# A two-block network on one Trainium2 core: other filler beside the RWKV recurrence, and linear attention's rows kept on chip

## The chip, the cores and the metric
The kernel runs on one core of a Trainium2 chip. The core has five engines, each with its own queue of instructions that it works off in order: TensorE (PE; its weight loads are shown apart as PEld), VectorE (DVE), ScalarE (ACT), GpSimd (POOL) and SyncE (SP), which issues most of the transfers. Engines wait for each other through semaphores. The metric is device time of one execution in microseconds (us); the profile of one execution gives its span from the first to the last instruction.

## The reference
Two blocks over 512 tokens of width 1024, in float32:

```python
# first block
p = rmsnorm(x, norm1_g) @ w_in
p_rwkv, q, k, v, gate_logits = jnp.split(p, IN_SPLITS, axis=-1)
y_a = rwkv7_bidirectional(p_rwkv, ...) @ w_o_rwkv
y_b = neighbourhood_attention_2d(q, k, v, q_gain, k_gain, rpb) @ w_o_na
g_a, g_b = jnp.split(jax.nn.sigmoid(gate_logits + b_gate), 2, axis=-1)
x = x + (g_a * y_a + g_b * y_b) @ w_out
x = x + hierarchical_moe(rmsnorm(x, norm2_g), ...)
# second block; the six modulation vectors depend on c and w_mod alone
sh1, sc1, g1, sh2, sc2, g2 = split(silu(c) @ w_mod + b_mod)
z = modulate(rmsnorm_2(x), sh1, sc1) @ w_in          # hyena | GLA | GDN
y = concat([hyena_mix(...), gla_branch(...), gdn_branch(...)]) @ w_out
x = x + g1 * y
x = x + g2 * sq_relu_mlp(modulate(rmsnorm_2(x), sh2, sc2), w1, w2)
```

`rwkv7_bidirectional` and the two branches GLA (linear attention with decays) and GDN (gated delta rule) are recurrences in chunks of 64 tokens; the neighbourhood attention lets each position of an 8 x 64 grid look at its neighbours.

## The kernel before
A matrix product in float32 precision is three matmuls of split operands (`gps<-hh,wh`, `hh,wl`, `hl,wh`, lines 293 to 295): ACT makes `wh` of a loaded weight tile `wraw` (L287), DVE makes the rest `wl` (L288). One projection of 128 output columns over 512 tokens takes one weight load of 512 KB and 24 matmuls of 128x512. A gate is such a projection and a Tanh on ACT.

The order of work is made by generators. `weave` takes streams with weights and always advances the one that has done least for its weight; a stream's `yield` says how much it has just done. A third number gives its instructions a high priority. So an engine's queue holds a recurrence's serial steps with other work, the filler, between them. Each queue is in order, SP's too: a transfer that waits for its data holds those behind it.

`block1_in` (from 26 to 517 us) weaves `rwkv` at 800 with `fill` at 120. `fill` does the projections of the attention (`na_proj`, which also writes q, k and v to DRAM), and after them the modulation vectors (`mods`: 48 loads of 512 KB, matmuls `mps`). The RWKV's inverses pass small matrices through DRAM (`nd`, `qd`, on SP). The last y of the RWKV is made on POOL (L631) and stored by SP to `yad` (L632).

`block1_out` weaves `na_attn` at 90, with priority, and `mix_a` at 104. `na_attn` loads the gains `qg`, the values `vb` (eight loads of 256 KB, L765), then for four pairs of heads `qkx` and `qksq` (L770, L773), and for each of 16 blocks a bias `bm`, scores `sp` (L795), softmax, transposes `pt` (L809) and the product with the values `yv` (L815). `mix_a` makes gates 8 to 15 and stores them to `gd`, loads `yad`, and makes gates 0 to 7, each followed by its part of the product with `w_o_rwkv`; its transfers are issued by ACT.

In the second block `mixer_in` runs from about 1260 to 1728 us. `side_proj` makes 28 projections: nine for the GDN, whose convolutions run on DVE, seven for the linear attention (`gk`, `gq`, `gv`), then gates and hyena's input. `early` pulls the first nine, beside `prep` (the GDN's gates, q, k, v) and `gla_flags`. Then `chain`, the GDN's scan, at 192 runs beside the rest of `side_proj` at 108. Behind it `gla_general` reads a flag into registers of all engines and loops zero or one time over a general form of the linear attention: zero times for usual inputs, in which case it is a branch at which all engines meet. Then `gla` at 112, `head_norm_out` of the GDN at 36 and hyena at 88 are woven. `gla` adds its chunks (`aop`) into rows that lie in DRAM (`oad`): for each of 16 pieces a load of `Oa` (L1641), an add and a store (L1643). At the end `mixer_out` weaves `head_norm_out` of the linear attention, which loads these rows back as `hO` (L1940, eight loads), with the output product.

## Time and profile before

| | us |
|---|---|
| median of three runs | 2209.9 (2203.88 to 2212.68) |
| the profiled execution | 2204.94 |
| its span | 2203.1 |

The mean granted clock of TensorE over the span is 0.937, where 1.0 is 2.4 GHz and 0.5 is 1.2 GHz, the two levels. A window's row in the trace gives its length, the busy time of each engine, the mean granted clock and the share and rate of the DMA engines. Work in full-speed microseconds is PE's busy time by the clock, and the rest of a window is loss: idle time, and what the lower level costs.

### The profile page before, as it was taken

The numbers are of one execution on the slowest core, as the hardware profiler recorded it, in microseconds if no ns is written. First come the engines' busy times: TensorE is split into PE (matmuls) and PEld (weight loads), VectorE is DVE, ScalarE is ACT, GpSimd is POOL, SyncE is SP. The second block draws the span as 40 slices with busy tenths as digits, with TensorE's granted clock in tenths as the row PEclk, the third lists the DMA queues.
The fourth block names the chain that finished last, engine by engine and source line by source line (L and its number), as shares of the span: only waits on it lengthen the run. The fifth ranks groups of instructions, "written<-read, shape, count | busy, mean of one in ns | idle before, by whom it ended". The sixth has DMA issues, their size and how long they took to land. (4 is left out here: it accounts for less than half of the span.)

```text
span 2203.1 us, 37817 instructions
## 1 busy us (share of the span) xinstructions
PE 1932.0 (88%) x15280; PEld 1410.3 (64%) x15280; DVE 1131.0 (51%) x2542; ACT 720.1 (33%) x1390; POOL 241.3 (11%) x246
## 2 busy tenths in 40 slices
PE   7999999887599789998999487899879689999997
PEld 5877776645367575444524265676567477898897
DVE  4665656532352445454361477776556475433433
ACT  3433333212262343121322365422252124312321
POOL 0101010000000201111000032310011150000000
PEclk9999999988799989999999798999989899999998
DMA  5222122565634638978796532241152532333332
GB/s 157 77 58 59 48 64 73 176 210 169 189 102 121 202 119 300 319 295 286 266 316 209 218 106 86 87 116 53 61 184 72 179 110 88 95 96 96 95 90 74
DMA packets 180723, 315.35 MB, mean 143 GB/s; under 512 B 77640, under 2 KB 98904, under 8 KB 180538
## 3 DMA queue, kind: packets, MB, share of 16 engines
q1 hardware_dynamic: 170746, 290.79, 41.6%
q10 hardware_dynamic: 5184, 13.63, 2.0%
q0 software_dynamic: 4608, 8.40, 1.1%
q8 instruction: 123, 2.02, 0.4%
q14 instruction: 62, 0.51, 0.1%
HBM read 279.80 MB, written 41.35 MB: 146 GB/s over the span
## 5 line engine op out<-in xcount | busy, mean ns | idle before, releaser
L288 DVE TENSOR_TENSOR wl<-wraw,wh 128x1024 fp32r<-128x1024 f32 (+2 forms) x215 | 221.8, 1033 | 250.2 <-ACT wh L287 249.6
L287 ACT ACTIVATE wh<-wraw 128x512 fp32r<-128x512 f32 (+2 forms) x233 | 195.9, 844 | 285.1 <-PE gpt L326 145.4
L293 PE MATMUL gps<-hh,wh 128*128 128x512 f32 x568 | 234.7, 414 | 10.6 <-issue 9.2
L294 PE MATMUL gps<-hh,wl 128*128 128x512 f32 x568 | 232.9, 411 | 0.5 <-DVE wl L288 0.3
L295 PE MATMUL gps<-hl,wh 128*128 128x512 f32 x568 | 231.8, 409 | 0.0
L324 PE MATMUL gpt<-wh,mh 128*128 128x256 f32 x512 | 142.9, 279 | 0.0
L325 PE MATMUL gpt<-wl,mh 128*128 128x256 f32 x512 | 142.9, 279 | 0.0
L326 PE MATMUL gpt<-wh,ml 128*128 128x256 f32 x512 | 142.9, 279 | 0.0
L1175 PE MATMUL hps<-w,xT 128*64 128x512 f32 x512 | 140.4, 605 | 2.1 <-DMA w<-in_w_moe 2.1
L293 PEld LDWEIGHTS gps<-hh,wh 128*128 128x128 f32 x568 | 108.9, 192 | 38.7 <-issue 12.5
L294 PEld LDWEIGHTS gps<-hh,wl 128*128 128x128 f32 x568 | 108.8, 192 | 30.2 <-issue 3.6
L295 PEld LDWEIGHTS gps<-hl,wh 128*128 128x128 f32 x568 | 108.6, 191 | 25.1 <-issue 1.9
L293 PE MATMUL gps<-lhh,wh 128*128 128x512 f32 x232 | 98.2, 426 | 6.2 <-ACT cpad L1267 4.6
L294 PE MATMUL gps<-lhh,wl 128*128 128x512 f32 x232 | 97.9, 424 | 5.5 <-DVE wl L288 3.9
L324 PEld LDWEIGHTS gpt<-wh,mh 128*128 128x128 f32 x512 | 96.2, 188 | 0.1
L325 PEld LDWEIGHTS gpt<-wl,mh 128*128 128x128 f32 x512 | 96.2, 188 | 0.1
L295 PE MATMUL gps<-lhl,wh 128*128 128x512 f32 x232 | 96.2, 417 | 0.0
L326 PEld LDWEIGHTS gpt<-wh,ml 128*128 128x128 f32 x512 | 96.2, 188 | 0.0
L2001 POOL TENSOR_TENSOR x<-x,xev 128x512 f32<-128x512 f32 x36 | 50.4, 1405 | 404.8 <-DVE xev L1999 356.9
L1175 PEld LDWEIGHTS hps<-w,xT 128*64 128x64 f32 x512 | 36.6, 137 | 63.4 <-issue 50.3
L1276 DVE SCALAR_TENSOR_TENSOR cout<-cpad,cw,cout 128x512 f32<-128x512 f32 (+1 forms) x90 | 68.5, 761 | 2.0
L324 PE MATMUL gpt<-wh,uh 128*128 128x256 f32 x224 | 65.1, 290 | 3.8 <-ACT uh L825 2.2
(1175 smaller groups left out, 4132.3 us busy)
## 6 DMA issues: line engine op xcount, KB each, us to landing
w<-in_w_moe SPq DMA_DIRECT2D x192, 512.0 KB
wraw<-in_w_modb SPq DMA_DIRECT2D x48, 512.0 KB
wraw<-in_w_in_2b SPq DMA_DIRECT2D x41, 512.0 KB
wraw<-in_w_mlp1b SPq DMA_DIRECT2D x32, 512.0 KB
wraw<-in_w_mlp2b SPq DMA_DIRECT2D x32, 512.0 KB
wraw<-in_w_inb SPq DMA_DIRECT2D x23, 512.0 KB
wraw<-in_w_inb ACTq DMA_DIRECT2D x16, 512.0 KB
bm<-in_c_bias SPq DMA_DIRECT2D x16, 256.0 KB
```

The source lines that it names most:

```text
L287: nc.scalar.activation(wh, raw[:, o:o + g], AF.Copy)
L288: self.we.tensor_sub(wl, raw[:, o:o + g], wh)
L293: nc.tensor.matmul(ps, wh, hh, start=first, stop=False)
L294: nc.tensor.matmul(ps, wl, hh, start=False, stop=False)
L295: nc.tensor.matmul(ps, wh, hl, start=False, stop=last)
L324: nc.tensor.matmul(ps, hh[:, g, sl], wh[:, k], start=f, stop=False, skip_group_check=True)
L325: nc.tensor.matmul(ps, hh[:, g, sl], wl[:, k], start=False, stop=False, skip_group_check=True)
L326: nc.tensor.matmul(ps, hl[:, g, sl], wh[:, k], start=False, stop=l, skip_group_check=True)
L1175: nc.tensor.matmul(ps[q], xT[:, 4 * kh + k, q], self.parts[h][:, 512 * (k - 2 * c):512 * (k - 2 * c) + 512], start=kh == 0 and k == 0, sto ...
L1276: nc.vector.scalar_tensor_tensor(ov[:n], pv[:n, :, j:j + L], wcol[:n, j:j + 1], ov[:n], op0=OP.mult, op1=OP.add)
L2001: (nc.gpsimd if last is None or cb < 3 else nc.vector).tensor_add(o, o, t)
```

## The change
It has three parts. First, `fill` weaves `na_proj` with `mods` from the start, and then makes gates 8 to 15 (new generator `gates`, whose stores SP issues); its weight goes from 120 to 160. `mix_a` loses these gates and has 64 instead of 104; `bg`, the gates' bias, is loaded at the start. Second, the eight loads of `vb` are issued by GpSimd instead of SP. Third, in the second block, `oad` is loaded once into a tile `oa` while the scan runs, `gla` adds into it, and `head_norm_out` reads it; the transfers Oa and the eight loads hO of `oad` go. `early` pulls the first 16 projections instead of nine, its weight is 96 instead of 54, the rest runs beside the scan at 66 instead of 108, and `gla_general` with its branch stands ahead of the scan.

```diff
 # na_attn
-                nc.sync.dma_start(vb[:, b, g, :], self.vd[...])
+                nc.gpsimd.dma_start(vb[:, b, g, :], self.vd[...])
+    def gates(self):
+        for j in range(8):
+            g = self.fl.tile([128, T], F32, name="st", bufs=2)
+            self.gate(8 + j, g)
+            self.nc.sync.dma_start(self.gd[j], g)
+            yield 5
 # mix_a
-        self.bg = self.cvec("bg", self.A["b_gate"][0], 2048, self.mp)
-        nc.vector.tensor_scalar(self.bg, self.bg, 0.5, None, op0=OP.mult)
-        for j in range(8):
-            g = self.mt.tile([128, T], F32, name="gld", bufs=2)
-            self.gate(8 + j, g)
-            self.dq.dma_start(self.gd[j], g)
-            yield 5
 # block1_in
-                yield from self.na_proj()
-                yield from self.mods()
-            self.run(self.weave((self.rwkv(), 800), (fill(), 120)))
+                yield from self.weave((self.na_proj(), 62), (self.mods(), 55))
+                yield from self.gates()
+            self.bg = self.cvec("bg", self.A["b_gate"][0], 2048)
+            self.nc.vector.tensor_scalar(self.bg, self.bg, 0.5, None, op0=OP.mult)
+            self.run(self.weave((self.rwkv(), 800), (fill(), 160)))
 # block1_out
-                self.run(self.weave((self.na_attn(), 90, 1000000), (....mix_a(), 104)))
+                self.run(self.weave((self.na_attn(), 90, 1000000), (....mix_a(), 64)))
 # gla
-                    O = pool.tile([128, 192], F32, name="Oa", bufs=3)
-                    nc.sync.dma_start(O, od[c, :, 192 * hp:192 * hp + 192])
+                    O = od[:, c, 192 * hp:192 * hp + 192]
                     nc.vector.tensor_add(O, O, op.rearrange("p h d -> p (h d)"))
-                    nc.sync.dma_start(od[c, :, 192 * hp:192 * hp + 192], O)
 # head_norm_out
-        O = pool.tile([128, 8, 384], F32, name="hO")
-        for c in (0, 7, 1, 6, 2, 5, 3, 4):
-            nc.sync.dma_start(O[:, c], od[c])
+        if O is None:
+            (as before)
 # mixer_in
-                    while not w.there.issuperset(GDN_BLOCKS):
+                    while not w.there.issuperset(SIDE_BLOCKS[:16]):
-                    self.run(self.weave((early(), 54), (prep(), 60), (v.gla_flags(8, gf), 20)))
+                    self.run(self.weave((early(), 96), (prep(), 60), (v.gla_flags(8, gf), 20)))
+                with tp(name="gz", bufs=1) as ga:
+                    v.gla_general(8, ga, lambda n: load(ga, self.gpd[n], "lsc"), self.oad)
-                    self.run(self.weave((chain(), 192), (side, 108)))
+                    self.run(self.weave((chain(), 192), (side, 66)))
+                    self.oa = self.ox.enter_context(tp(name="oa", bufs=1, side="right")).tile([128, 8, 384], F32, name="oa")
+                    nc.sync.dma_start(self.oa, self.oad.rearrange("c p d -> p c d"))
-            with tp(name="gz", bufs=1) as ga:
-                v.gla_general(8, ga, lambda n: load(ga, self.gpd[n], "lsc"), self.oad)
 # mixer_out
-                self.run(self.weave((self.head_norm_out(pool, self.oad, 3, self.agng, 2), 18), (side(), 28)))
+                self.run(self.weave((self.head_norm_out(pool, None, 3, self.agng, 2, self.oa), 18), (side(), 28)))
```

Before the change, SP's queue between the RWKV and the attention ends a run of parameter loads (`gng` is the last) and goes on so; `yad` is the store of y:

```order
L1978 DMA gng<-in_gdn_norm_g 96x1
L632 DMA yad<-y 128x512
L220 DMA bg<-in_b_gate 128x16x1
L758 DMA qg<-in_q_gain 64x1 x2
L758 DMA qg<-in_k_gain 64x1 x2
L765 DMA vb<-vd 128x1x512 x8
L770 DMA qkx<-qkd 128x512
```

With the change the same stretch of SP's queue is this; `gd` are the stores of gates from the fill, `rnd` the attention's norms:

```order
L749 DMA rnd<-nrt 64x128
L282 DMA wraw<-in_w_inb 128x1024
L837 DMA gd<-st 128x512 x2
L632 DMA yad<-y 128x512
L758 DMA qg<-in_q_gain 64x1 x2
L758 DMA qg<-in_k_gain 64x1 x2
L770 DMA qkx<-qkd 128x512
L773 DMA qksq<-rnd 64x512 x2
```

The parameter loads and vb are gone from between y and qkx: vb stands in POOL's queue behind the last y, and the parameter loads come later in SP's queue, among the biases bm.

At the end of the mixer SP's queue before the change holds the gate rows `hsg`, the residual `x`, the rows of the linear attention `hO`, the mixed rows `uld` and the output weights:

```order
L1935 DMA hsg_16740<-sgd 128x512
L225 DMA g1r<-mdd 128x1024
L1992 DMA x_16718<-x1d 128x1024 x4
L1940 DMA hO<-oad 128x384 x8
L2176 DMA uld<-mixd 128x512 x2
L282 DMA wraw<-in_w_out_2h 128x512 x3
```

With the change SP's queue at that place is:

```order
L225 DMA g1r<-mdd 128x1024
L1994 DMA x_16675<-x1d 128x1024 x4
L1936 DMA hsg_16693<-sgd 128x512
L1936 DMA hsg_16695<-sgd 128x512
L1936 DMA hsg_16697<-sgd 128x512
L2180 DMA uld<-mixd 128x512 x2
L282 DMA wraw<-in_w_out_2h 128x512 x3
```

The eight loads hO are gone, and the loads of x and hsg have changed places.

On PE the flag's read (TENSOR_LOAD `aflag`) stands before the change right behind the scan, whose last matmuls are `gop`; `ttp` and `zp` belong to the loop that runs zero times:

```order
L1501 MATMUL gop<-vn__14793,E_13104 64x96 x2
L1499 MATMUL gop<-gSn,qT__12000 64x96 x2
L1501 MATMUL gop<-vn__14800,E_13104 64x96 x2
L1688 TENSOR_LOAD aflag
L1689 COMPARE_AND_BRANCH
```

With the change PE reads it between the early projections (`gps<-lhh`) and the scan:

```order
L1381 MATMUL tcp<-ct_58,kv_12668 96x128 x8
L295 MATMUL gps<-lhl,wh 128x512
L293 MATMUL gps<-lhh,wh 128x512
L294 MATMUL gps<-lhh,wl 128x512
L295 MATMUL gps<-lhl,wh 128x512
L1689 TENSOR_LOAD aflag
L1690 COMPARE_AND_BRANCH
```

The branch has moved ahead of the whole scan, and nothing parts the scan's end from the linear attention.

## Rows read from the trace of the kernel before

**Rows 1.** Page, part 1: busy us, share and instructions by engine
```profile
PE 1932.0 (88%) x15280; PEld 1410.3 (64%) x15280; DVE 1131.0 (51%) x2542; ACT 720.1 (33%) x1390; POOL 241.3 (11%) x246
```

**Rows 2.** Windows of the first block: length, busy by engine, PEclk, DMA, GB/s
```profile
26.00:400.00 374.00, 362.46 (x4325) 279.43 (x4323) 225.78 (x530) 128.58 (x231) 43.32 (x36) 1.00 0.26 68
400.00:517.40 117.40, 99.03 (x1465) 60.00 (x1461) 43.71 (x137) 24.50 (x60) 7.03 (x6) 0.91 0.65 193
517.40:580.00 62.60, 29.04 (x112) 23.11 (x113) 14.07 (x21) 12.68 (x16) 1.26 (x1) 0.72 0.61 184
580.00:648.00 68.00, 67.98 (x361) 43.59 (x362) 40.85 (x113) 44.19 (x121) 0.00 (x0) 0.91 0.48 147
648.00:712.00 64.00, 63.69 (x277) 49.85 (x275) 18.85 (x25) 17.44 (x29) 0.00 (x0) 1.00 0.35 97
```

**Rows 3.** SP's queue, 505 to 575: start us, us, line, transfer
```profile
533.36 3.73 SPq L1978 DMA_DIRECT2D gng<-in_gdn_norm_g  x6
537.19 0.37 SPq L632 DMA_DIRECT2D yad<-y  x1
...
542.36 17.82 SPq L765 DMA_DIRECT2D vb<-vd  x8
560.22 2.56 SPq L770 DMA_DIRECT2D qkx<-qkd  x1
...
564.06 0.58 SPq L770 DMA_DIRECT2D qkx<-qkd  x1
571.03 0.45 SPq L773 DMA_DIRECT2D qksq<-rnd  x1
```

**Rows 4.** Timeline at the RWKV's end and the first scores
```profile
515.67 1.70 PE L432 MATMUL ynp<-ct,ynb 128*128 128x128 f32 x7
...
519.03 1.26 POOL L631 TENSOR_TENSOR y<-y,gt 128x512 f32<-128x512 f32 x1 [6.05 <-DVE y L630]
...
580.02 0.76 PE L795 MATMUL sp__5743<-qkn,qkn 64*128 64x256 f32 x1 [23.04 <-issue]
```

**Rows 5.** DMA issues (count, KB, us to landing); POOL's issues, min/median/max ns
```profile
wraw<-in_w_modb SPq DMA_DIRECT2D x48, 512.0 KB
...
xg<-h2d,gi POOLq DMA_INDIRECT x16, 7.3
...
L1147 POOL DMA_INDIRECT xg<-h2d,gi x16: 988/1028/1210, 829.1 to 1131.9; - x16
```

**Rows 6.** The page's costliest groups: DVE's split of a weight tile
```profile
L288 DVE TENSOR_TENSOR wl<-wraw,wh 128x1024 fp32r<-128x1024 f32 (+2 forms) x215 | 221.8, 1033 | 250.2 <-ACT wh L287 249.6
```

**Rows 7.** Windows of the second block
```profile
1260.00:1400.00 140.00, 116.23 (x569) 88.92 (x568) 102.78 (x184) 84.17 (x152) 34.32 (x44) 0.90 0.30 96
1400.00:1590.00 190.00, 181.58 (x1774) 129.11 (x1772) 132.26 (x357) 52.56 (x122) 24.58 (x28) 1.00 0.27 76
1590.00:1625.00 35.00, 19.38 (x107) 12.41 (x106) 7.52 (x18) 13.95 (x30) 0.00 (x0) 0.67 0.60 199
1625.00:1728.00 103.00, 92.92 (x845) 74.06 (x846) 72.18 (x180) 33.40 (x69) 19.07 (x18) 0.95 0.30 89
1728.00:1760.00 32.00, 15.06 (x83) 10.77 (x84) 9.21 (x15) 7.51 (x16) 1.69 (x2) 0.68 0.74 253
```

**Rows 8.** Chain of waits at the mixer's end: start us, us, what
```profile
1732.00 8.02 DMA x<-x1d
1740.04 6.37 DMA hO<-oad
1746.43 4.38 DMA wraw<-in_w_out_2h
```

**Rows 9.** Groups of PE, 1727 to 1760 us
```profile
L1947 PE MATMUL ops<-hO,ct 128*64 128x384 f32 x16 | 7.3, 674 | 15.3 <-DMA hO<-oad 15.3
```

**Rows 10.** Timeline at the branch behind the scan
```profile
1592.07 0.26 DVE L1503 TENSOR_TENSOR Og<-Og,gop 128x96 f32<-128x96 f32 x1 [0.77 <-ACT Og L1502]
...
1599.80 0.15 DVE L1610 TENSOR_SCALAR aok<-anok 128x1 f32<-128x1 f32 x1 [7.48 <-DMA ogd<-Og]
```

More of the change, by code (lines that the diff above doesn't have):

```diff
@@ L764, in na_attn @@
                 k0 = (0, 8, 24, 32)[b]
-                nc.sync.dma_start(vb[:, b, g, :], self.vd[256 * g:256 * g + 256].rearrange("(r k) c -> r k c", k=64)[:, k0:k0 + 32])
+                nc.gpsimd.dma_start(vb[:, b, g, :], self.vd[256 * g:256 * g + 256].rearrange("(r k) c -> r k c", k=64)[:, k0:k0 + 32])
         for hp in range(4):
@@ L923, in block1_out @@
             with tp(name="nt", bufs=1) as self.nt:
-                self.run(self.weave((self.na_attn(), 90, 1000000), (self.view({}, dq=self.nc.scalar).mix_a(), 104)))
+                self.run(self.weave((self.na_attn(), 90, 1000000), (self.view({}, dq=self.nc.scalar).mix_a(), 64)))
             self.hpx.close()
@@ L1927, in side_proj, with head_norm_out @@
             yield 6
-    def head_norm_out(self, pool, od, gate, gcol, j0):
+    def head_norm_out(self, pool, od, gate, gcol, j0, O=None):
         nc, C = self.nc, self.C
@@ L1937, in head_norm_out @@
         yt = pool.tile([128, 4, 4, 96], F32, name="hyt")
-        O = pool.tile([128, 8, 384], F32, name="hO")
-        for c in (0, 7, 1, 6, 2, 5, 3, 4):
-            nc.sync.dma_start(O[:, c], od[c])
+        if O is None:
+            O = pool.tile([128, 8, 384], F32, name="hO")
+            for c in (0, 7, 1, 6, 2, 5, 3, 4):
+                nc.sync.dma_start(O[:, c], od[c])
         ss = pool.tile([128, 4, 4], F32, name="hss")
@@ L2084, in mixer_begin @@
         tp = self.tc.tile_pool
-        self.far = ExitStack()
+        self.far, self.ox = ExitStack(), ExitStack()
         w = self.w = self.view(dict(p="g", s="g", i="p"), wg=512)
@@ L2157, in hyena @@
                         yield from u.hyena(hp, 1)
-            with tp(name="gz", bufs=1) as ga:
-                v.gla_general(8, ga, lambda n: load(ga, self.gpd[n], "lsc"), self.oad)
             with tp(name="ga", bufs=1) as ga, tp(name="hn", bufs=1) as hn:
                 un = self.view(dict(p="i"))
-                self.run(self.weave((v.gla(8, False, ga, lambda n: load(ga, self.gpd[n], "lsc"), self.oad), 112),
+                self.run(self.weave((v.gla(8, False, ga, lambda n: load(ga, self.gpd[n], "lsc"), self.oa), 112),
                                     (un.head_norm_out(hn, self.ogd, 0, self.gng, 5), 36), (hyena(), 88)))
@@ L2189, in mixer_out @@
             with tp(name="hn", bufs=1) as pool:
-                self.run(self.weave((self.head_norm_out(pool, self.oad, 3, self.agng, 2), 18), (side(), 28)))
+                self.run(self.weave((self.head_norm_out(pool, None, 3, self.agng, 2, self.oa), 18), (side(), 28)))
+            self.ox.close()
             for k in range(3):
```

## The prediction

> **What bounds the kernel now.** I read the share of each engine first: TensorE (PE) is busy 88% of the span and no other engine is over 51% [rows 1], so time can only come from stretches in which PE waits or runs at its lower clock. I then cut the span into stages and took, for each, PE's busy time by the mean granted clock; what is left of the stage I call loss. The reader is to see five rows of the first block [rows 2]. From 26 to 400 us: 374 us, work 362.5, loss 11.5. From 400 to 517.4, where the modulation vectors are the filler: 117.4 us, work 99.03 x 0.91 = 90.1, loss 27.3, with the DMAs moving 193 GB/s against 68. From 517.4 to 580: 62.6 us in which PE does 112 matmuls; at 0.23 us each (63.69 us for 277 at full clock) that is 25.8 of work and 36.8 of loss. From 580 to 648: loss 6.1. From 648 to 712: loss 0.3. So the hole is between the RWKV's last matmul, which ends at 517.4, and the first scores matmul at 580.02 [rows 4]. The work in SyncE's (SP's) queue explains it [rows 3]: y is ready at 520.29 [rows 4], its store stands behind parameter loads and is issued at 537.19, then come eight loads of vb for 17.82 us, and the first qkx only at 560.22. In the second block the losses stand in the same table [rows 7]: 35.4 from 1260 to 1400, 8.4 from 1400 to 1590, 22.0 from 1590 to 1625, 14.7 from 1625 to 1728, 21.8 from 1728 to 1760.
>
> **First part: the fill of the RWKV stage.** Eight gates move from mix_a into the fill. A gate is 24 matmuls, 24 x 0.23 = 5.52 us. By the order of instructions, 4.67 of them now lie before the RWKV's last norm matmul and 68 matmuls (15.6 us) between it and the first scores. Work up to that matmul: 362.5 + 90.1 + 4.67 x 5.52 = 478.4. The loss is unknown. The nearest row for a stage whose last stretch has dense filler is the first one, 11.5 in 374; the modulation loads (48 of 512 KB [rows 5]) are now spread over the whole stage instead of 117 us. Below it can hardly come under 14 (the row's rate over 491 us is 15), above it stays at the 38.8 of both stretches. I take 20, nearer to the lower end, since the dense matmuls now stand where the clock was 0.91. The stage then ends at 26 + 478.4 + 20 = 524.4 instead of 517.4: this part by itself is paid for with 7 us.
>
> **The transition.** Work left from there to the end of mix_a: before 25.8 + 67.98 x 0.91 + 63.7 = 151.4 in 194.6 us; after 151.4 - 25.8 = 125.6. The loss has three terms. (1) Waiting for the first scores. y ends 2.9 us after the last norm matmul [rows 4]. The parameter loads are no longer ahead of its store. From that store's issue to vb's took 5.2 us (537.19 to 542.36), from qkx's issue to the first scores 19.8 us (560.22 to 580.02) [rows 3, 4]: together 25 with vb's bytes still in the way. SP stood 6.4 us before the third qksq at 571.03 (the second qkx issue ends at 564.64); without it, 18.6. I take 20, nearer the lower end since vb's issue itself is gone from the queue. The 15.6 us of gates lie in it, so PE idles 2.9 + 20 - 15.6 = 7.3 (5.9 to 12.3). (2) The attention's window: 6.1 before; mix_a gives less filler, but ACT is busy 44.19 of 68 us there and does not bind. I take 6; it would be 18 if the window kept its 68 us with about 12 us of filler less, and 3 at the best. (3) The lower clock after the idle time: 2. Sum 125.6 + 15.3 = 140.9, so mix_a ends at 665.3 instead of 712: **a gain of 46.7**, with the 7 us of the first part paid.
>
> **vb on GpSimd's queue.** The program of before has only gathers and scatters there: 1.03 us of GpSimd for each issue, 7.3 us to landing [rows 5]. Eight issues are 8.2 us, the last lands about 15.6 us after y. The first use comes after the scores, so I price it at nothing, covered by the 20 us above; without that cover it is a few us. The rows show that the issue of eight loads held SP for 17.82 us [rows 3]. The Trainium skill, page DMA: Bandwidth & Descriptors, section Issuing engines are not separate DMA queues, says that transfers from any engine run on the same 16 DMA engines and that another issuer saves only issue time, usually small beside the transfer. Here the issue was not small; if by that rule only the bytes counted, the first scores would stand at the 25 us end, 5 us later.
>
> **Second block.** (a) The rows of the linear attention stay on chip. Before, the chain at its end is x<-x1d 8.02, hO<-oad 6.37, wraw<-in_w_out_2h 4.38 [rows 8], and PE waits 15.3 for hO [rows 9]. The eight loads (1.5 MB) go; at the row's 253 GB/s that is 6 us. x and the weights are still late next, so of 15.3 at most, I take 8. The 32 transfers Oa<->oad also go, and one load of 1.5 MB goes in beside the chain, where the DMAs are 27% busy; from 1625 to 1728 PE loses 14.7, of which I take 2 (0 to 5). (b) The branch on a flag, at which all engines meet, moves from behind the scan to ahead of it. It cost from the last Og at 1592.07 to 1599.80 [rows 10], 7.7 us; at the new place it must drain too, and I put 8 against it (4 to 14, since the stretch behind it refills). Net 0. (c) Seven projection blocks (7 x 5.52 = 38.6 us of PE) move from the chain's stretch to the early one. Early has 35.4 of loss to fill, but its DVE is 73% busy and each block adds 1.03 us there [rows 6, 7]; half of the 38.6 fits into loss, 19.3 lengthens it. The chain gets shorter by 38.6 less what it then lacks as filler: 16 taken. Net gain 3 (from -12 to +15). Sum of the block: 8 + 2 + 0 + 3 = **13** (-12 to 30).
>
> **Sum.** 2204.9 - 46.7 - 13 = 2145 us, against the profiled execution's own 2204.94; the median of the runs, 2209.9, stands 0.2% above that and I leave the forecast on the profiled one.
>
> **Rivals.**
> - The chain starves. With 12 blocks of filler instead of 19 and a meeting of all engines ahead of it, the scan's serial steps show. For it: in 1400 to 1590 PE is 181.58 of 190 busy with a third fewer fillers to come. Against: DVE is 132.26 of 190 [rows 7], not at its limit. Then (c) gives -12 and (b) -10: 13 becomes -12, time 2170.
> - vb is late. GpSimd must write each load itself; if each of the eight waits for one wl on DVE, 1.03 us [rows 6], they take 16.5 us and land 24 us after y, 8 us after what (1) grants if the first use came at once: 2153. The Trainium skill, SBUF — State Buffer, section SBUF: two separate sides, has such a rule: DVE in certain modes locks GpSimd out of a shared port and its DMAs then wait for descriptors; no run here shows that yet.
> - The gates do not fill. If the inverse's small transfers through DRAM stand behind waiting weight loads in SP's queue, the RWKV keeps the lost time and adds to it: stage loss 60 instead of 20, 2185. The change then hardly does what it says.
> - Slower. The same place with the modulation loads: if the rate of 400 to 517.4 (27.3 in 117.4, 0.23 a us) held for the whole 491 us, the loss would be 114 instead of 20, time 2145 + 94 = 2239. It turns slower from a loss of 80, a rate of 0.16. Against it: the same 25 MB spread over four times the length brings the DMAs from 68 to some 120 GB/s, not to 193 [rows 2].
>
> **How the numbers follow.** The forecast has 0.63 (with 0.08 in it for a better case, 2112, in which early takes all moved blocks), the starved chain 0.13, late vb 0.07, gates that do not fill 0.09, slower 0.05; 0.03 is left for no change. All low ends together give 2118, all high ends 2206. The range 2110 to 2188 leaves out the last two cases and some of the ends. About 0.5% is what a measurement of this kernel tells from no change, 2199 and below being faster: faster 0.91, same 0.04, slower 0.05.
>
> **What would show it.** Right: the first scores some 23 us after the RWKV's last norm matmul, no row of PE idle over 10 us there; qkx issued within 6 us of y's store; mix_a's end near 665; no wait for hO at the end of the mixer. Wrong: mps or the inverse's matmuls waiting on DMA all through the first 500 us; the first yv waiting for vb; PE under 90% busy in the scan's stretch; a stall of over 15 us at the flag's new place.

## The result

The changed kernel takes 2179.0 us in the median of four runs (2176.3 to 2193.3), against 2210.2 before (2203.9 to 2212.7): a ratio of 0.988, interval 0.984 to 0.992. Eight more executions gave 2184.0 against 2206.0, 0.990 (0.986 to 0.993). Medians here and below are of all executions; the ratios leave out those over 1.5% longer than the fastest of the same kernel (one of e1, one of the second set of e2, two of e13, one of the kernel before). The forecast was 2145, range 2110 to 2188: the direction was right, the size was not. 60 us were forecast (46.7 and 13); 31 came in the first set and 22 in the second.

The profiled execution has a span of 2175.4 us, 27.7 less than the one before, and a mean granted clock of 0.932, against 0.937. Its first part reads:

```profile
PE 1954.9 (90%) x15280; PEld 1427.1 (66%) x15280; DVE 1136.3 (52%) x2542; ACT 719.2 (33%) x1390; POOL 245.5 (11%) x254
```

PE is busy 90% of the span, against 88% [rows 1], with the same 15280 matmuls. Where the 27.7 us come from is seen by putting the same events of both traces side by side; the last column is what each stretch gained or lost.

| event on PE | before | after | gain of the stretch |
|---|---|---|---|
| RWKV's last norm matmul ends | 517.4 | 542.7 | -25.3 |
| mix_a's last matmul ends | 711.9 | 695.6 | 41.6 |
| first projection of the second block | 1255.4 | 1236.4 | 2.7 |
| the scan's last matmul ends | 1591.6 | 1599.0 | -26.4 |
| first product of the linear attention (aop) | 1649.1 | 1640.9 | 15.6 |
| its last aop ends | 1729.3 | 1718.9 | 2.2 |
| its last rows go through the head norm (ops) | 1753.0 | 1723.5 | 19.1 |
| end of the span | 2203.1 | 2175.4 | -1.8 |

So in this pair of traces the first block gives 16.3 by mix_a's end, the rows on chip and the moved branch give 37, and the stretch of early projections and scan takes 26 back. The 16.3 is a good execution: ten traces hold this first block unchanged (the whole change twice, e1, e2 twice, e7, e8, e10, e11 and e13, all explained below), and in them mix_a ends between 692.5 and 716.2, at 702 in the mean. Against the one trace of before that is 10 us.

**The first block after.** Windows of the changed kernel, columns as in [rows 2]:

```profile
26.00:400.00 374.00, 354.75 (x4184) 264.68 (x4186) 207.26 (x481) 116.37 (x210) 34.09 (x29) 0.96 0.36 100
400.00:542.70 142.70, 137.20 (x1711) 98.09 (x1700) 71.47 (x186) 45.80 (x92) 13.02 (x11) 0.99 0.36 103
542.70:570.80 28.10, 15.49 (x71) 12.48 (x69) 8.42 (x12) 6.14 (x9) 6.94 (x9) 0.81 0.81 152
570.80:644.80 74.00, 67.69 (x357) 43.42 (x357) 43.94 (x121) 43.46 (x121) 1.42 (x2) 0.86 0.72 201
644.80:695.60 50.80, 50.75 (x212) 39.21 (x212) 14.18 (x18) 14.60 (x23) 0.00 (x0) 1.00 0.32 91
```

From 26 to 400 us the loss is now 374 - 354.75 x 0.96 = 33, where [rows 2] had 11.5; from 400 to the stage's end it is 7, where it had been 27. The loss has moved to the front of the stage and is in sum what it was, some 39 us. Counted as in the prediction, the stretch to the first scores loses 28.1 - 71 x 0.23 = 12 us instead of 36.8 (PE stands still for 12.6), and the attention's window loses 74 - 67.69 x 0.86 = 16 instead of 6. In that window PE is idle for 6.3 us and the rest of the loss is the lower level; before, it was never idle there.

SP's queue, POOL, DVE and PE at the transition, from the timeline of the changed kernel, beside [rows 3] and [rows 4]:

```profile
544.41 1.29 POOL L631 TENSOR_TENSOR y<-y,gt 128x512 f32<-128x512 f32 x1 [43.23 <-issue]
548.91 5.65 POOL L765 DMA_DIRECT2D vb<-vd  x8 [3.21 <-DMA yad<-y]
...
545.77 0.38 SPq L632 DMA_DIRECT2D yad<-y  x1
...
550.63 0.58 SPq L770 DMA_DIRECT2D qkx<-qkd  x1
...
561.81 0.49 DVE L780 TENSOR_SCALAR qkx<-qkx,qg 128x512 f32<-128x512 f32 x1 [6.30 <-DMA qkx<-qkd]
...
569.82 0.75 DVE L778 SCALAR_TENSOR_TENSOR qkn<-qkx,qg,qksq 128x512 f32<-128x512 f32 x1 [4.68 <-DMA qksq<-rnd]
...
570.78 0.76 PE L795 MATMUL sp__6030<-qkn,qkn 64*128 64x256 f32 x1 [12.61 <-issue]
```

y is ready at 545.7, its store is issued at once (17 us later before), and qkx 5 us after it, as forecast. But qkx takes 11 us to arrive and the last qksq 14, and the first scores come 25.1 us after y, not 20. The eight loads of vb, all issued within 5.65 us, are in flight beside them, as the tile's rows show (the last line is the time from issue to landing):

```profile
L765 POOL DMA_DIRECT2D vb<-vd x8: 677/677/931, 548.9 to 553.9; - x8
...
DMA to landing us min/median/max: 13.0/18.0/23.5
```

**The second block after.** Windows, columns as in [rows 7]:

```profile
1236.40:1400.00 163.60, 142.95 (x696) 111.24 (x695) 117.68 (x219) 97.08 (x174) 34.84 (x45) 0.93 0.34 105
1400.00:1420.00 20.00, 14.02 (x121) 8.98 (x122) 10.33 (x17) 4.88 (x9) 6.49 (x8) 0.83 0.15 45
1420.00:1523.00 103.00, 96.31 (x1093) 74.70 (x1089) 76.95 (x179) 24.11 (x49) 17.29 (x20) 1.00 0.33 85
1523.00:1599.00 76.00, 73.58 (x471) 47.19 (x470) 36.94 (x141) 16.01 (x50) 0.00 (x0) 0.50 0.16 54
1599.00:1641.00 42.00, 38.02 (x306) 31.46 (x308) 23.81 (x55) 28.62 (x57) 5.67 (x4) 0.89 0.64 207
1641.00:1719.00 78.00, 73.95 (x654) 54.01 (x654) 55.15 (x142) 17.40 (x39) 14.06 (x14) 0.98 0.13 41
1719.00:1751.00 32.00, 19.78 (x118) 16.39 (x119) 22.51 (x44) 10.71 (x19) 7.77 (x6) 0.79 0.76 258
```

The fourth row is the one to see. In the scan PE is busy 73.58 of 76 us, at a granted clock of 0.50, the lower of its two levels: counted as in the prediction, half of its busy time, 37 us, is lost to the level. That is an upper bound, since the small matmuls do not take twice as long: 96 of the matmuls gop (96x96) take 14.8 us of PE here, and 80 took 7.9 at full clock, 1.6 times as long each. Before, [rows 7], the whole stretch from 1400 to 1590 was at 1.00. The branch, now in the second row, costs about 8 us (20 - 14.02 x 0.83). Behind the scan the linear attention starts after 42 us instead of 57.5.

At the mixer's end the chain of waits of the changed kernel is short; it stands beside [rows 8], with the PE group that answers to [rows 9] below it:

```profile
1719.03 4.15 DMA g1r<-mdd
1723.20 7.06 DMA uld<-mixd
```

```profile
L1950 PE MATMUL ops<-oa,ct 128*64 128x384 f32 x16 | 5.6, 492 | 0.5 <-DVE oa L1644 0.5
```

The wait of 15.3 us for hO is gone; PE waits 0.5 us for the last add into the rows. What is late next is the residual's row of gains and the mixed rows, 11 us together, part of which PE fills.

### The profile page after: what moved, and what is told of

It reads as the page before. It is cut to its first block, busy times and chain, and to the rows that moved or that the text cites. A ratio compares the mean times of both kernels' runs of the same rounds, so it can differ in the third digit from the quotient of the medians.

```text
span 2175.4 us, 37783 instructions
## 1 busy us (share of the span) xinstructions
PE 1954.9 (90%) x15280; PEld 1427.1 (66%) x15280; DVE 1136.3 (52%) x2542; ACT 719.2 (33%) x1390; POOL 245.5 (11%) x254
## 5 line engine op out<-in xcount | busy, mean ns | idle before, releaser
L288 DVE TENSOR_TENSOR wl<-wraw,wh 128x1024 fp32r<-128x1024 f32 (+2 forms) x215 | 227.9, 1062 | 235.7 <-ACT wh L287 235.3
L324 PE MATMUL gpt<-wh,mh 128*128 128x256 f32 x512 | 142.9, 279 | 0.0
L325 PE MATMUL gpt<-wl,mh 128*128 128x256 f32 x512 | 142.9, 279 | 0.0
L326 PE MATMUL gpt<-wh,ml 128*128 128x256 f32 x512 | 142.9, 279 | 0.0
L1178 PEld LDWEIGHTS hps<-w,xT 128*64 128x64 f32 x512 | 36.9, 138 | 66.2 <-issue 50.8
L2019 DVE TENSOR_TENSOR uld<-uld 128x512 f32<-128x512 f32 x32 | 22.2, 693 | 87.3 <-ACT uld L2018 87.3
```

Of the source, the lines that this page charges most:

```text
L288: self.we.tensor_sub(wl, raw[:, o:o + g], wh)
L324: nc.tensor.matmul(ps, hh[:, g, sl], wh[:, k], start=f, stop=False, skip_group_check=True)
L325: nc.tensor.matmul(ps, hh[:, g, sl], wl[:, k], start=False, stop=False, skip_group_check=True)
L326: nc.tensor.matmul(ps, hl[:, g, sl], wh[:, k], start=False, stop=l, skip_group_check=True)
L1178: nc.tensor.matmul(ps[q], xT[:, 4 * kh + k, q], self.parts[h][:, 512 * (k - 2 * c):512 * (k - 2 * c) + 512], start=kh == 0 and k == 0, sto ...
L2019: nc.vector.tensor_mul(f, f, f)
```

## The experiments

A cell of the table is the median of the kernel, the number of executions, and the ratio to the kernel before with its interval. The rows are explained one by one below. Diffs are shortened; lines in words stand for several.

| kernel | median us | runs | ratio |
|---|---|---|---|
| whole change | 2179.0 / 2184.0 | 4 / 8 | 0.988 (0.984 to 0.992) / 0.990 (0.986 to 0.993) |
| e1 first block alone | 2196.2 | 10 | 0.997 (0.994 to 1.000) |
| e2 and rows on chip | 2180.8 / 2179.5 | 4 / 6 | 0.986 (0.978 to 0.994) / 0.989 (0.985 to 0.994) |
| e7 and projections early, branch behind | 2200.4 | 10 | 0.996 (0.994 to 0.999) |
| e3 fill in sequence | 2180.9 | 4 | 0.988 (0.984 to 0.993) |
| e4 vb spread | 2181.0 | 4 | 0.987 (0.983 to 0.992) |
| e6 vb on SP | 2186.9 | 5 | 0.991 (0.988 to 0.995) |
| e9 gates back | 2187.8 | 10 | 0.993 (0.990 to 0.996) |
| e14 fill at 220 | 2193.1 | 7 | 0.995 (0.992 to 0.998) |
| e8 dense work in the scan | 2229.7 | 5 | 1.009 (1.006 to 1.013) |
| e10 filler held | 2228.9 | 4 | 1.012 (1.005 to 1.019) |
| e12 filler held, vb spread | 2219.5 | 10 | 1.007 (1.004 to 1.011) |
| e11 rows on chip, filler held | 2205.4 | 10 | 1.004 (1.000 to 1.007) |
| e13 branch in the middle | 2191.1 | 10 | 0.994 (0.990 to 0.998) |
| e15 rows on chip, vb spread | 2179.2 | 6 | 0.990 (0.986 to 0.993) |

### The second block, part by part

The first block alone, with the second as before:

```diff
-SIDE_BLOCKS[:16], weights 96 and 66, gla_general ahead of the scan, rows in oa
+GDN_BLOCKS, weights 54 and 108, gla_general behind the scan, rows in DRAM
```

> The change's first block alone (fill with gates, vb on GpSimd's queue, weights), the second block as before. Theory: the traces give 19 us up to the first latent projection (1255.4 before, 1236.4 after) and the rest of the second block only 9, so this kernel takes 19 less than before, 2191, and its scan runs at full clock again. Rival: the first block's gain is worth more, and what is lost in the second block is a consequence of it (transfers or buffers that come at other times); then this kernel is near 2183 or its scan is slow too.

Its profiled execution needs 336.4 us from the first projection to the scan's end, as the kernel before did, and the scan is at full clock:

```profile
1233.80:1400.00 166.20, 141.14 (x823) 106.47 (x824) 125.37 (x230) 96.31 (x172) 45.94 (x55) 0.91 0.28 91
1400.00:1504.00 104.00, 99.18 (x1069) 73.78 (x1063) 72.83 (x188) 25.81 (x56) 12.71 (x8) 1.00 0.32 86
1504.00:1570.20 66.20, 64.04 (x488) 42.26 (x487) 41.30 (x135) 19.46 (x52) 0.74 (x10) 0.98 0.19 64
```

So the slow scan belongs to the third part of the change. The profiled execution, 2177.9, was this kernel's fastest of ten; eight of the others lie between 2188.1 and 2208.7, each with a lower mean clock (0.946 at 2177.9, 0.933 at 2208.7). In the median the first block is worth about 10 us, not the 19 that two traces show, and the interval of the ratio goes from 14 us to nothing.

Then the rows on chip, with nothing else of the third part:

```diff
-(early(), 96), (side, 66), SIDE_BLOCKS[:16], gla_general ahead of the scan
+(early(), 54), (side, 108), GDN_BLOCKS, gla_general and the load of oa behind the scan
```

> The change's first block, and in the second block only the rows kept on chip (loaded behind the branch); early projections, weights and the branch as before. Theory: the 26 us that the traces lose between the first latent projection and the scan's end come from the seven moved projections, and the rows on chip bring 19 at the mixer's end and 2 in the linear attention: 21 less than the kernel with the first block alone, about 2170, with the scan at full clock. Rival: the rows on chip cost as much where they are loaded or the gain at the end is the branch's: no more than 8 less than the first block alone, 2183.

The median is 15.4 under the first block alone, with executions that lie 31 us apart; the traces say it more firmly. In its profile 142.9 us lie between the scan's end and the last head norm, against 158.1 in e1, and 143.3 in a second trace of the same kernel: the rows on chip are worth 15, half as much again as the 10 that the sum had. The theory's full clock did not come: the second trace has 31 us of the scan at 0.50, and in this execution too the scan fell to the lower level for a part:

```profile
1515.40:1546.10 30.70, 30.50 (x155) 18.50 (x154) 13.51 (x48) 4.82 (x14) 0.15 (x2) 0.50 0.12 39
1546.10:1596.50 50.40, 48.67 (x359) 32.38 (x357) 30.05 (x95) 15.07 (x39) 0.59 (x8) 1.00 0.17 60
```

The trace of e15, which has the same second block, holds 1.00 through all of the scan. The four executions of e2 lie at 2164 and 2168 with a mean clock of 0.950 and 0.946, and at 2193 and 2195 with 0.936 and 0.933.

Now the seven projections early, with the branch still behind the scan:

```diff
-v.gla_general(...) between early and the scan, the load of oa beside the scan
+v.gla_general(...) behind the scan, then the load of oa
```

> The whole change, but the branch at which all engines meet stands behind the scan again; the seven projections stay early. Theory (too little filler is left for the scan, whose small matmuls then run at the lower clock): the scan stays at 0.5 for over 60 us, and the time is 5 to 12 longer than with the whole change, 2184 to 2191, since the 16 us gained between scan and linear attention are lost against 6 at the new place. Rival (the meeting ahead of the scan upsets its order): the scan is at full clock and the time is some 15 below the whole change, 2164.

```profile
1247.00:1410.00 163.00, 143.24 (x700) 111.99 (x700) 117.27 (x219) 96.97 (x174) 34.49 (x44) 0.93 0.33 105
1410.00:1529.70 119.70, 109.50 (x1210) 83.71 (x1208) 87.74 (x195) 29.03 (x58) 24.55 (x28) 0.99 0.30 80
1529.70:1604.60 74.90, 72.51 (x465) 46.58 (x463) 36.44 (x139) 15.74 (x50) 0.00 (x0) 0.50 0.11 34
```

The scan is at 0.50 without the branch ahead of it, so it is the moved projections and not the meeting of the engines that does it. The other traces agree: over the last 76 us of the scan the mean clock is 0.50 to 0.64 in all eight traces with the seven projections early (the whole change twice, e3, e4, e6, e7, e9, e14) and 0.83 to 1.00 in the five without (the kernel before, e1, e2 twice, e15). The price is 2200.4 against 2180.8 for e2, about 20 us lost, where the sum had 3 gained; from the first projection to the scan's end the traces say 7 to 22 (357.6 here, 351.1 and 349.8 in e2, 336.0 in e15).

The branch's move is worth 16 to 21 us in the medians (2200.4 against 2184.0 and 2179.0), where the sum had put it at nothing: in the traces 17.3 us less lie between the scan's end and the last head norm (141.8 in e7, 124.5 in the whole change), against 5 more ahead of it. The load of oa moves with it; no add waits for it in e7, but a load of the linear attention beside it (lsc) holds ACT for 5.4 us, so a part of the 17 may be the load's. The two halves of the rearrangement cancel.

To see whether the branch can be had without the price, it went between the solving stage and the scan:

```diff
+self.run(self.weave((solve(), 68), (nine projections, 48)))
+v.gla_general(...)
+self.run(self.weave((gdn_scan(...), 124), (the rest, 60)))
```

> The change's first block and rows on chip; nine early projections as before; the branch at which all engines meet stands between the solving stage and the scan, with nine projections as filler ahead of it and ten behind it (two buffers of the branch's loop share memory, so that it fits). Theory (the branch is cheap in the middle, some 6 us against 17 behind the scan, and the moved projections are what starves the chain): the chain has its filler as before, from the first latent projection to the scan's end about 342 to 350, and from there to the last output rows of the linear attention 125 as in the whole change; time 2160 to 2170, below the whole change and below the rows on chip alone. Rival (all engines meeting is as dear here, since the solving stage and the scan are both bound by their own chain and the stage empties): 2175 to 2190.

2191.1, the rival. PE does 13.67 us in the 20 around the meeting, and behind it the level is 0.51 for 30 us (windows around the branch):

```profile
1470.00:1490.00 20.00, 13.67 (x287) 12.07 (x286) 9.34 (x11) 4.23 (x6) 2.97 (x1) 0.97 0.32 69
1490.00:1520.00 30.00, 29.54 (x150) 16.90 (x146) 10.98 (x42) 6.15 (x17) 0.00 (x0) 0.51 0.02 8
```

From the first projection to the scan's end it takes 361.2 us, not 342 to 350. And 136.3 us lie between the scan's end and the last head norm, not 125, though the branch stands ahead of the scan here too: the branch alone does not set that stretch. What else does is not shown.

### Why the scan is slow

One matmul for each head and step, 96x512, out of the scan's rows; its result is read by nothing:

```diff
+hot = self.ps.tile([128, 512], F32, name="hot", tag="g", bufs=2)
+nc.tensor.matmul(hot[0:96], x, self.xwarm, start=True, stop=True)
```

> The whole change with one matmul more for each head and step of the scan, 96x512 in float32 out of the scan's own rows (so that it can't be moved ahead of it), 32 in all, whose result nothing reads. Theory (the scan is slow because PE falls to the lower clock for want of dense work): the clock holds at 1.0 in the scan, and although 32 matmuls of 0.5 us are added, the stretch from 1523 to the scan's end becomes 10 to 20 us shorter than the 76 us of the whole change; time some 2165. Rival (the scan waits for its own chain of DVE and ACT, and the clock follows from that): the stretch gets longer by up to 16 us, time 2185 to 2195.

```profile
1420.00:1523.00 103.00, 76.73 (x1000) 57.97 (x1001) 62.51 (x147) 15.59 (x31) 21.10 (x14) 0.82 0.25 60
1523.00:1650.40 127.40, 125.00 (x721) 72.22 (x719) 54.96 (x181) 26.89 (x73) 0.74 (x10) 0.87 0.17 56
```

The mean clock in the scan rose from 0.50 to 0.87, as the theory has it, and the kernel became some 50 us slower all the same: the added matmuls show as 64 records of about 0.67 us, some 43 us, and since they take turns in the PSUM buffers of the projections these came late too (76.73 busy of 103 in the stage ahead). PE was busy 98% of the scan's stretch, against 97% in the whole change. What differs is what it did beside the scan's own matmuls: 53 records of the added ones and 48 triples of projection matmuls, against 11 projection matmuls in the whole change. The run does not tell the added matmuls from the late projections, and it shows no way to win by them.

The same PSUM turn, with one matmul of 8 columns per step, was then used to hold the projections for the scan:

```diff
+if od is not None and i == 0:
+    hot = self.ps.tile([128, 512], F32, name="hot", tag="g", bufs=2)
+    nc.tensor.matmul(hot[0:96, 0:8], x, self.xwarm[:, 0:8], start=True, stop=True)
+def paced():             # the projections: slower ahead of the scan, faster in it
+    for n in side:
+        yield n * (1.1 if "scan" in st else 0.85)
-self.run(self.weave((chain(), 192), (side, 66)))
+self.run(self.weave((chain(), 192), (paced(), 66)))
```

> The whole change, with the same 12 projections of filler beside the scan's stage, but held for the scan: at each of its eight steps one matmul of 8 columns out of the scan's own rows takes a turn of the PSUM buffers that the projections use, so that PE can't take them all in the stage ahead. By the order of instructions 45 triples of projection matmuls lie ahead of the scan's first state update and 40 among its steps, where the whole change has 77 and 8. Theory (the scan runs at the lower clock because its filler is used up ahead of it): the scan is at 1.0 but for short falls, and from the first latent projection to the scan's end it takes 10 to 25 us less than the 362.6 of the whole change; time 2155 to 2170. Rival (the stage ahead needs the filler as much as the scan does): the stage ahead idles or falls to the lower clock instead, and the time stays within 8 of the whole change's.

2228.9: the rival, and worse than it. The windows of the solving stage and of the scan, and under them two of the longest waits from 1420 to 1530 (total, times, longest):

```profile
1420.00:1500.00 80.00, 63.74 (x711) 49.43 (x711) 51.85 (x109) 16.77 (x31) 17.31 (x13) 0.89 0.28 75
1500.00:1648.90 148.90, 129.75 (x975) 87.67 (x976) 68.87 (x223) 27.16 (x75) 3.71 (x11) 0.71 0.17 51
```

```profile
POOL qv L673 <- DMA qc<-qd: 21.8, 2, 12.9
...
PE ips L684 <- DVE qv L673: 14.9, 2, 13.2
```

In the solving stage the inverse sends small matrices through DRAM, and with 45 triples of projections instead of 77 PE stands still for 13.2 us over such a hop. Nor did 40 triples keep the scan at the higher level; it has 0.71. From the first projection to the scan's end it takes 394.1 us instead of 362.6. The theory that the projections need only be held for the scan falls.

> The first block changed, rows on chip, nine early projections and the branch behind the scan, with the filler held for the scan: 60 triples ahead of its first state update and 56 among its steps, against 69 and 47 without the holding matmuls. Theory: the clock no longer falls in the scan in some executions, so the median comes near the fastest run without holding, 2164. Rival: it falls ahead of the scan instead and the median stays near 2181.

The same holding on e2 (with 1.3 and 0.7 for 1.1 and 0.85) gave 2205.4 against 2180, worse than the rival. Its windows of the solving stage and of the scan:

```profile
1400.00:1480.00 80.00, 64.79 (x792) 51.68 (x793) 49.68 (x118) 16.73 (x31) 12.85 (x8) 0.94 0.38 97
1480.00:1610.10 130.10, 126.14 (x823) 83.47 (x820) 64.49 (x207) 30.44 (x80) 0.74 (x10) 0.81 0.15 50
```

Here no projection had been moved out of the chain, and still PE stands in the solving stage and the scan is at 0.81; from the first projection to the scan's end it takes 375.8 us instead of 351.1 and 349.8. So the holding costs some 25 us by itself, and the loss of e10 can't be put down to the moved projections: whether 12 projections could serve both stages with a better means of holding them is not shown. And with vb spread, on e10:

> The kernel with the held filler and vb's loads spread behind the biases. Theory: the spread gave 2 us by the end of the attention's stage, and nothing takes it back: 0 to 5 below the kernel with the held filler alone. Rival: the transfers of the attention's stage are bound by their bytes, and it is the same within 2 or slower.

2219.5 against 2228.9, more than the theory had; the two kernels differ in the first block by 6 us already at mix_a's end (716.2 and 710.4 in the profiles), and executions of the same first block lie further apart than that (below), so no more is read into it.

### The first block, part by part

The gates back in the attention's stage:

```diff
-                yield from self.gates()
+        for j in range(8):          # in mix_a, as before
+            self.gate(8 + j, g)
```

> The whole change, but gates 8 to 15 are made in the attention's stage again (fill at 120, that stage's other stream at 104); the fill's order, vb's queue and the second block as changed. Theory (the gates' matmuls cost the same wherever they are, and what was gained is the wait for the first scores): the RWKV's last norm matmul ends some 20 to 25 us earlier, near 520, and the end of that stage comes within 5 us of the 695.6 of the whole change. Rival (the gates fill idle time of the recurrence, so moving them is the gain): the end of the stage comes 10 to 25 us later than 695.6.

```profile
26.00:516.40 490.40, 459.82 (x5772) 341.81 (x5770) 269.95 (x648) 152.03 (x289) 49.36 (x40) 0.97 0.34 95
516.40:701.60 185.20, 164.10 (x761) 117.89 (x761) 77.50 (x175) 74.70 (x167) 8.32 (x11) 0.92 0.57 158
```

The RWKV's stage ends 26 us earlier and mix_a 6 us later (701.6 against 695.6): between the two accounts, nearer to the first. The gates cost nearly their whole work in the RWKV's stage. Moving them is worth 4 to 9 in the medians, with intervals that overlap, and 701.6 lies among the ten traces of the changed first block (692.5 to 716.2): that it gains at all is not clear of the noise.

vb on SP's queue again:

```diff
-                nc.gpsimd.dma_start(vb[:, b, g, :], ...)
+                nc.sync.dma_start(vb[:, b, g, :], ...)
```

> The whole change, but vb is loaded on SP's queue again, between y's store and qkx. Theory (only the bytes matter): the first scores come within 4 us of where the whole change has them, 25 us after y. Rival (the queue matters): qkx is issued about 12 to 18 us later than with the whole change, and the first scores come 37 to 43 us after y.

```profile
556.34 12.69 SPq L765 DMA_DIRECT2D vb<-vd  x8
569.08 2.48 SPq L770 DMA_DIRECT2D qkx<-qkd  x1
```

The queue matters: from y's store qkx is issued 12.7 us later, and the first scores come at 588.6, 37 us after y (551.4), against 25.1 to 28.4 in the ten traces with the loads on GpSimd. What the kernel gains by it is less sure: in the median it is 3 to 8 slower here, with intervals that overlap, and mix_a's end, 705.1, lies among those ten.

vb spread behind the biases, so that it does not travel beside the first qkx:

```diff
-            nc.gpsimd.dma_start(vb[:, b, g, :], ...)         # all eight, ahead of the first qkx
+                for g in range(2 if hp == 0 else 0):         # two behind each bias
+                    nc.sync.dma_start(vb[:, b, g, :], ...)
```

> The whole change, but the eight loads of vb are spread: two behind each bias of the first pair of heads, on SP's queue. Theory (vb's 2 MB take the bandwidth from qkx, qksq and bm, so the first scores came 25 us after y and the attention's first blocks waited): qkx lands within 5 us of its issue instead of 11, the first scores come 14 to 18 us after y, the attention ends 5 to 10 us earlier relative to the RWKV's last norm matmul (102 us with the whole change). Rival (the transfers are slow for another reason, or the first product with the values then waits): the first scores stay at 25 or the time from the last norm matmul to the attention's end stays at 102 or grows.

```profile
555.11 0.58 SPq L766 DMA_DIRECT2D qkx<-qkd  x1
...
571.39 4.66 SPq L787 DMA_DIRECT2D vb<-vd  x3
576.10 2.52 SPq L766 DMA_DIRECT2D qkx<-qkd  x1
```

The first scores come 13.1 us after y instead of 25.1, so vb's bytes did hold them. But the attention ends 100.5 us after the last norm matmul against 102.1, and the median does not move: vb now stands ahead of the next pair's qkx. That the stage is bound by its bytes is not shown by this: from 570.8 to 644.8 the DMAs of the changed kernel move 201 GB/s, where [rows 2] had 147, but PE's waits there, 6.2 us in all, are for DVE (the softmax's m and s, and wl) and none is for a transfer. With the rows on chip it is the same kernel again:

> The same with vb's loads spread behind the biases. Theory: the attention's stage is bound by the bytes it loads, so it is the same within 0.3%. Rival: 5 to 10 us faster, and then faster than both kernels.

2179.2, and without the spread:

> The first block changed, rows on chip, early projections and branch as before, once more with more executions. Theory (the moved projections and the moved branch cancel, so that the rows on chip carry the second block's gain): the same as the whole change within 0.5%, 2172 to 2190, with some executions near 2165 in which the scan holds its clock. Rival: without the moved projections it is faster by more than 0.5%, under 2170.

2179.5. Nothing here beats the changed kernel by more than can be measured.

The order of the fill:

```diff
-                yield from self.weave((self.na_proj(), 62), (self.mods(), 55))
+                yield from self.na_proj()
+                yield from self.mods()
```

> The whole change, but the fill is again first the attention's projections, then the modulation vectors, then the gates. Theory (the early modulation vectors leave the recurrence too thin a filler, the clock falls at 304 to 325 us): that stretch is at full clock, the RWKV's last norm matmul ends 5 to 12 us earlier than with the whole change, about 533 instead of 542.7. Rival (the loss belongs to the recurrence, or to where the modulation loads crowd the transfers): the loss only moves to where the loads now are, the end of the stage stays within 4 us of 542.7, or is later.

The stage ends at 546.1 and the time is the same: weaving the modulation vectors in early is worth nothing by itself. The stretch from 280 to 350 is at 0.88 here and at 0.85 in the whole change; what lowers it can't be told from that, since the vectors run from 294 to 490 us here and so lie in it too. The fill's weight was tried last:

```diff
-(fill(), 160)
+(fill(), 220)
```

> The whole change with the fill beside the RWKV at 220 instead of 160, so that the gates' matmuls come earlier. Theory (the loss of 39 us in that stage comes from a recurrence that has little dense filler at 280 to 350, while the gates bunch at the end): 280 to 350 us loses 8 us less, and the RWKV's last norm matmul ends 5 to 10 us earlier than 542.7. Rival (the loss belongs to the recurrence and moves to wherever filler is thin): the stage ends within 4 us of 542.7 or later, with the loss now at its end.

Windows from 280 to 350 of the changed kernel and of e11, whose first block is the same; then of this kernel, from 280 to 350 and behind the stage:

```profile
280.00:350.00 70.00, 66.96 (x766) 47.29 (x766) 35.76 (x87) 19.10 (x38) 7.42 (x6) 0.85 0.31 89
```

```profile
280.00:350.00 70.00, 66.50 (x893) 49.62 (x893) 37.35 (x91) 21.32 (x41) 7.45 (x7) 1.00 0.33 95
```

```profile
280.00:350.00 70.00, 67.48 (x766) 49.27 (x765) 35.22 (x83) 20.20 (x36) 6.82 (x6) 0.98 0.39 121
...
560.70:594.70 34.00, 9.31 (x31) 6.85 (x31) 8.12 (x13) 5.62 (x8) 6.92 (x9) 0.60 0.79 175
```

With 110 projection matmuls in that stretch instead of 64 its clock is 0.98, a loss of 4 instead of 13. That thin filler was the cause is not shown by it: e11 has 76 of them and is at 1.00, and among the ten traces of the changed first block the stretch is anywhere from 0.78 to 1.00. The loss of the whole stage stays at 40. What the weight does change is the end: no gates are left for the wait behind the stage, PE does 9.31 us in 34 there, the first scores come 31 us after y, and the median is 9 us above that of the whole change's second set.

### The changed kernel once more

> The whole change once more, beside the other kernels of this call. Every account expects 2176 to 2193 as in its first runs; the scan at the lower clock for over 60 us and the RWKV's last norm matmul at 540 to 550 if what its first trace shows is its usual course, and other places if the falls of the clock come and go between executions.

```profile
1528.60:1604.40 75.80, 73.38 (x471) 47.21 (x470) 36.82 (x141) 16.04 (x50) 0.00 (x0) 0.50 0.17 54
```

The scan's lower level came again over the same 76 us. The RWKV's stage ended at 548.0 and mix_a at 705.4, ten later than in the first trace, with nothing changed in the code. In the ten traces of this first block the stage ends between 540.0 and 553.6 and mix_a between 692.5 and 716.2. What is read there from one pair of traces is good to no better than that; waits inside the transition, such as that from y to the first scores, repeat to some 3 us.

## Why the prediction failed

**The work was right, the loss was not.** The RWKV's stage was to hold 478.4 us of work and holds 477; the stretch to mix_a's end 125.6 and holds 125.3 (71 matmuls at 0.23 us up to the first scores, then 58.2 and 50.8). What was counted from the first block's instructions stands. The losses were 19 and 12 us above what was taken, and these are the 30 us by which mix_a's end, 695.6, missed 665.3.

**Loss beside the RWKV: 20 taken, 39 measured.** The step that failed is the choice of the end: the row of 11.5 in 374 was taken as what dense filler brings, and the loss of 27 under the modulation vectors as something that spreading would dissolve. It did not dissolve: 33 now lie ahead of 400 us, and the sum is what it was. No order, number or weight of the filler that was tried lowered it: the stage's loss is 41 with the fill in sequence (e3), 43 with the gates back (e9), 40 at weight 220 (e14), and 33 to 49 in the ten traces of the changed first block. Why the stage loses some 40 us stays open. The third rival, gates that do not fill, lies nearest in its number, but its mechanism is not seen: PE's waits for a modulation load sum to 4.3 us in the stage, against 10.4 before. The upper end of the range, 38.8, was the right value.

**The transition: 15.3 of loss taken, 28 measured.** SP's part came as worked out (5 us from the store to qkx, 17 us of parameter loads gone). The 20 us to the first scores became 25.1, the bound with vb's bytes in the way, and PE stood still for 12.6 instead of 7.3. The window of the attention lost 16, where 6 and 2 for the clock had been taken: the lower level lasts on after the longer wait and takes over half of it, and for the rest, 6.3 us, PE was idle, nearly all of it waiting for DVE. Late vb, the second rival, did not come: nobody waits for vb in the trace. The rule cited from the Trainium skill, page DMA: Bandwidth & Descriptors, section Issuing engines are not separate DMA queues, has two halves here: that transfers of different issuers share the DMA engines is what e4 and the 25.1 us show; that the issuer's time is usually small is not so here, 12.69 us in e6. The other rule cited from the Trainium skill, page SBUF — State Buffer, section SBUF: two separate sides, is not seen: eight loads were issued in 5.65 us on GpSimd, less than the 8.2 worked out.

**The second block: 13 forecast, 9 measured, by other terms.** That the sum came near is luck. The rows on chip were worth 15 where 10 stood. The branch: the 7.7 us before its reopening were counted, but not the slow start behind it (22 us of loss from 1590 to 1625 in [rows 7]), so that 16 to 21 us, not 0, came with moving it. The seven projections: 3 gained became about 20 lost. That is the first rival, the starved chain, in its place but at the wrong price: I looked for waits and for DVE's limit, and the chain did not wait. PE stayed busy 73.58 of 76 us, at half the clock, so the sign that was named for it, PE under 90% busy in the scan's stretch, could not have shown it. The term was mis-sized since a filler matmul was valued at its own 0.23 us, and not at the level that the scan's own matmuls have with it and without it.

**The clock.** Span times mean clock is 2064 us before and 2027 after. If all time went with the clock, which the waits do not, the change would have saved 37 us at the higher level throughout, not 28; that is an estimate.

Three things stay open: what the 40 us of loss beside the RWKV are; why the same first block ends up to 24 us apart in different executions; and why the scan with the projections beside it holds the higher level throughout in the trace of e15 and falls for 31 us in both of e2, whose second block is the same.

## What to carry to other kernels

In this scan the filler had two values, the time it hid and the clock that the chain's own small matmuls had beside it; before moving filler out of a stretch that runs at 1.00, price the stretch at 0.50 too. The loss of the RWKV's stage stayed when its filler was rearranged, so take the measured loss of a whole stage as the first estimate. An edit made of several moves is measured move by move: here about 15, -20 and 16 to 21 us stood behind one small number. And before one trace is read against another, look at how far traces of the same code lie apart.

## What was not expected

- PE counted as busy hides the loss: in the scan it is busy 97% of 76 us in a stretch that runs at 0.50 throughout. Only the granted clock tells.
- The spread between executions goes with the clock. Nine executions of e1 go from 2177.9 (mean clock 0.946) to 2208.7 (0.933) in nearly the order of their clocks.
- Moving a branch that loops zero times, at which all engines meet, was worth 16 to 21 us where a slow start followed it, and it costs about 8 at its new place, between the early projections and the scan.
